# A second matrix product of an MLP by seven block products in place of eight, with the operand sums formed a stage earlier

## The chip, the cores and the metric

The kernel runs on one core of a Trainium2 chip. The metric is the device time of one execution in microseconds. All arithmetic results are float32; each large product is formed from float32 numbers that are split into a rounded part ("hi") and a remainder ("lo"), so that one 128x128 weight block against 128x512 tokens costs three matmuls: hi by hi, hi by lo, lo by hi.

## The reference, cut to what matters

The layer is a hybrid encoder (state-space heads and windowed attention), followed by an MLP. Only the MLP is touched. T is 2048 tokens, the model width 1024, the MLP width 4096:

```python
h = rmsnorm(x, norm_mlp_pre[i])
f = jnp.square(jax.nn.relu(h @ w_up[i])) @ w_down[i]
x = x + rmsnorm(f, norm_mlp_post[i])
```

## The kernel before

Activations lie transposed, features on the 128 partitions and tokens along the free axis. Tokens go in two halves `hf` of 1024, each of two blocks `b` of 512 (`TB`). The MLP has two stages.

The first product, `up`, runs for 2 halves times 16 units `p`. A unit computes two blocks of 128 MLP features for both token blocks. It is a 2x2 by 2x2 block product done with seven products (`PROD`: 1, 5, 6, 3, 7, 2, 4) of 12 matmuls each, whose partial results are chained in three PSUM banks x, y and z (`BANK`). `up_weights` makes the weights of each product: four raw loads for a unit, four of the seven weights formed by an add or subtract (`combine`; the letters of `wcmb='vvp'` say that two in three go to VectorE and one to GpSimd), then a cast to hi on ScalarE and a subtract to lo on VectorE. `up_input` forms the token operands of a half in the same way (`bcmb`, `blo`), in 16 slots of the tag "a" and 16 units of the tag "u". After its eviction each of the four results of a unit is squared (Relu, then Square, on ScalarE) and stored to the DRAM tensor `dff` by the queue of SyncE (SP).

The second product, `down`, runs for 2 halves times 4 quarters `qt` of the MLP width. For each of 8 output blocks `j` and both token blocks one `gemm` of 24 matmuls goes into a bank of the pool "g" (2 banks), and is then added on VectorE to `facc[j]` (copied by ScalarE in the first quarter). `ff_input` loads 16 tiles of `dff` for a quarter through five staging buffers (`stage`: two of tag "gl", three of tag "ld"), casts them to hi and subtracts to lo. Weights come through `wchunk`, two 256 KB chunks for each `j`. In the last quarter of a half `sqadd` adds up the squares of `facc` (ScalarE square, VectorE add), and `facc` is multiplied by `norm_mlp_post`. `final` then forms the norm and the residual and stores the output; for the first half it runs as a side task (`finals`) beside the first quarter of the second half. The very last quarter runs in three parts (`LAST`).

The order of TensorE is written out by hand: `drive` advances a clock of its own by 512/2400 us for a matmul and interleaves the main generator with side generators. The other engines' queues (SP, ScalarE, VectorE, GpSimd) are ordered by the framework's scheduler, and each runs its queue in order on the chip. A tile whose tag has no free buffer makes its first writer wait. Weights of a product are held in 4 buffers of the tag "ws". The tag "ct" has 5 buffers for results of `up`, "nt" has 4 and serves `sqadd` and the norms.

After half 1's normalisation begins (`post`), the units 0 to 3 of half 0 of `up` run beside the residual and norm work of the earlier stage, which uses "gl", "ld" and GpSimd.

Of the kernel before, what the change touches and what calls it, by code (L numbers as in the profile page):

```python
# [8 lines left out]
F32 = mybir.dt.float32  # L9
# [6 lines left out]
P = 128  # L16
D = 1024
# [20 lines left out]
class Layer:  # L38
    def __init__(self, ctx, tc, a, out):
# [24 lines left out]
        self.d_ff = d("dff", [32, P, T])  # L64
# [836 lines left out]
    def sqadd(self, acc, b, t, pool, tag):  # L901
        nc = self.nc
        if acc[b] is None:
            acc[b] = pool.tile([P, TB], F32, tag=tag, name=tag, bufs=2)[:, :t.shape[-1]]
            nc.scalar.activation(acc[b], t, AF.Square)
        else:
            q = self.nt("sq")[:, :t.shape[-1]]
            nc.scalar.activation(q, t, AF.Square)
            nc.vector.tensor_add(acc[b], acc[b], q)
# [53 lines left out]
    def up_weights(self):  # L963
# [3 lines left out]
        def load(p):  # L967
            raw = {}
            for i in range(2):
                for k in range(2):  # L970
                    t = raw[f"{i + 1}{k + 1}"] = self.pw.tile([P, 4, P], F32, tag="raw", name="wu", bufs=8)
                    nc.sync.dma_start(t, self.a["w_up"][2 * p + i, k])
            return raw
# [69 lines left out]
    def up(self, hf, p, B, ws):  # L1043
# [37 lines left out]
    def ff_input(self, hf, qt, ff, after):  # L1081


        nc = self.nc
        for b in range(2):
            for kt in range(8):
                if kt % 4 == 0 and after[b][kt // 4]:
                    yield self.until(after[b][kt // 4])
                x = self.stage(self.d_ff[8 * qt + kt, :, self.tok(hf, b)], kt)
# [3 lines left out]
                yield K["ff_prep"]  # L1093
            self.flags.add(f"ff{hf}{qt}{b}")
# [34 lines left out]
    def finals(self, parts, facc, facs):  # L1129
        for p, c in zip(parts, facs):  # L1130
            yield from self.final(0, p, facc, c, None, 0)

    def final(self, hf, part, facc, acc, xs, wait):
# [59 lines left out]
    def main(self):  # L1193
# [130 lines left out]
        ff = [[None, None] for _ in range(8)]  # L1324
        for hf in range(2):
            for p in range(16):
                if p == 8:
                    self.side(self.r2(hf))
                if p == 15:
                    if hf == 0:  # L1330
                        self.side(self.up_input(1, B[1]))
                    else:
                        self.side(self.ff_input(0, 0, ff, (("uB5", "uB6"), (None, "uB1"))))
# [4 lines left out]
        self.worder = [("w_down", j, (2 * qt, 2 * qt + 1)) for _ in range(2) for qt in range(4) for j in range(8)]  # L1338
        s6.close()
        self.pf, s7 = self.pool("f", "left", 8)  # L1340
        both = ((0, 0, TB), (1, 0, TB))
        for hf in range(2):
            facc = None
            for qt in range(4):
                yield self.until(f"ff{hf}{qt}0", f"ff{hf}{qt}1")
                if facc is None:
                    new = lambda: (self.unit("u", "facc", F32) if hf else
                                   self.pf.tile([P, 2, TB], F32, tag="f", name="facc"))
                    if hf:
                        self.side(self.finals(both, fa, facs))  # L1350
                    facc = [new() for _ in range(8)]
                cur, ff = ff, [[None, None] for _ in range(8)]
                n = (hf, qt + 1) if qt < 3 else (hf + 1, 0)
                if n[0] < 2:
                    self.side(self.ff_input(*n, ff, ((None, None), (f"dn{hf}{qt}1", None))))
                if qt == 3 and hf == 1:
                    ws, xs = [], None
                    yield self.until("fin000", "fin010")
                    for part in self.LAST:
                        facs = [None]  # L1360
                        yield from self.down(qt, cur, facc, (part,), facs, ws)
                        self.side(self.final(1, part, facc, facs[0], xs, K["fin_lag"]))
                        if xs is None:
                            xs = []
                            for j in range(8):
                                xs.append(self.unit("a", "x2", F32)[:, 0])
                                nc.sync.dma_start(xs[j], self.d_x2[j, :, self.tok(1, 1)])
                else:
                    facs = [None, None]
                    yield from self.down(qt, cur, facc, both, facs, None, f"dn{hf}{qt}")  # L1370
            fa = facc
# [85 lines left out]
```

## Time and profile before

| quantity | us |
|---|---|
| median of 3 runs | 3263.02 |
| range of these runs | 3262.8 to 3265.16 |
| profiled execution | 3271.05 |
| span of the profiled execution | 3269.3 |
| TensorE busy in the span | 3024.7 (93%) |
| VectorE busy | 1935.8 (59%) |
| ScalarE busy | 1457.4 (45%) |
| GpSimd busy | 844.6 (26%) |

The span runs from the first to the last instruction; 1.75 us lie around it. A stretch of 40 or of 20 us is better than the whole for judging a stage: `up` runs from about 1828 to 2523 us of the span, `down` from 2523 to about 3253 us. PEclk is the granted TensorE clock as a share of full speed. Since matmuls are pipelined, a busy share of TensorE says little; the count of matmuls in a stretch says more.

### The profile page before, as it was taken

How to read it: one execution, taken by the hardware profiler on the slowest of the kernel's cores; microseconds unless marked ns; L12 is line 12 of the kernel's file. 1: busy time of each engine (PE TensorE's matmuls, PEld its weight loads, DVE VectorE, ACT ScalarE, POOL GpSimd, SP SyncE). 2: the span in 40 equal slices, each digit the busy share in tenths (PEclk: the TensorE clock that was granted, in tenths of full speed). 3: DMA queues.
4: the chain of work that ended last, by engine and by line, in shares of the span. 5: the costliest groups of instructions: out<-in, count | busy, mean ns of one | idle time of the engine just before them, and what ended most of it. 6: DMA issues, size and time to landing. Idle time of an engine off the chain costs nothing. (4 is left out here: it accounts for less than half of the span.)

```text
span 3269.3 us, 40235 instructions
## 1 busy us (share of the span) xinstructions
PE 3024.7 (93%) x13896; PEld 2419.4 (74%) x13896; DVE 1935.8 (59%) x3292; ACT 1457.4 (45%) x2718; POOL 844.6 (26%) x710
## 2 busy tenths in 40 slices
PE   7989999999998899997988869999999999999996
PEld 6778887778886666674766658877888788877886
DVE  7365455557756689958778864565455333553346
ACT  3235566657765545322232545655566322332222
POOL 4242222222234345564536520022000000010001
PEclk9999999999999989997998989999999999999998
DMA  6767544464567655655348473332333422354323
GB/s 227 235 202 205 149 127 116 128 209 138 149 202 249 206 146 152 184 176 163 106 134 263 127 225 107 119 126 87 118 118 128 129 92 87 100 153 124 100 85 97
DMA packets 368955, 489.49 MB, mean 150 GB/s; under 512 B 30192, under 2 KB 198128, under 8 KB 368752
## 3 DMA queue, kind: packets, MB, share of 16 engines
q1 hardware_dynamic: 334128, 451.27, 46.0%
q10 hardware_dynamic: 34624, 35.66, 3.1%
q8 instruction: 110, 1.80, 0.2%
q14 instruction: 93, 0.76, 0.1%
HBM read 330.95 MB, written 155.86 MB: 149 GB/s over the span
## 5 line engine op out<-in xcount | busy, mean ns | idle before, releaser
L86 PE MATMUL psg<-ff,ws 128*128 128x512 f32 (+1 forms) x2760 | 626.1, 389 | 10.2 <-ACT facc L1105 9.0
L86 PEld LDWEIGHTS psg<-ff,ws 128*128 128x128 f32 x2760 | 515.3, 188 | 120.6 <-ACT facc L1105 11.9
L86 PE MATMUL psg<-h,ws 128*128 128x512 f32 x1920 | 486.4, 399 | 19.8 <-ACT z L470 18.0
L86 PEld LDWEIGHTS psg<-h,ws 128*128 128x128 f32 x1920 | 356.7, 190 | 93.7 <-issue 18.7
L84 PE MATMUL psmx<-b,ws 128*128 128x512 f32 x1152 | 297.0, 407 | 41.3 <-DVE c L1078 13.4
L218 POOL TENSOR_SCALAR ws<-wr 128x512 fp32r<-128x512 f32 x184 | 125.4, 682 | 749.2 <-PE psg L86 584.6
L84 PEld LDWEIGHTS psmx<-b,ws 128*128 128x128 f32 x1152 | 224.2, 196 | 98.9 <-ACT c L1075 9.4
L86 PE MATMUL psg<-hr,ws 128*128 128x512 f32 x960 | 250.4, 401 | 5.1 <-DMA hr<-dh 4.4
L221 POOL TENSOR_TENSOR ws<-wr,ws 128x512 fp32r<-128x512 f32 x184 | 250.0, 1359 | 14.7
L86 PE MATMUL psg<-ga,ws 128*128 128x512 f32 x768 | 209.0, 424 | 28.4 <-DVE mix L893 12.3
L777 DVE CUSTOM_DVE_ANT_0 p<-psqk,pack,sinks 128x384 f32<-128x384 f32 (+1 forms) x256 | 152.1, 596 | 139.0 <-PE psqk L86 138.4
L1153 POOL TENSOR_TENSOR facc<-facc,x 128x512 f32<-128x512 f32 (+1 forms) x20 | 24.5, 1223 | 753.8 <-DVE facc L1152 707.7
L86 PE MATMUL psg<-ya,ws 128*128 128x512 f32 x768 | 214.1, 420 | 3.3 <-DVE ya L201 3.2
L86 PEld LDWEIGHTS psg<-hr,ws 128*128 128x128 f32 x960 | 177.2, 190 | 42.3 <-DMA hr<-dh 7.3
L86 PEld LDWEIGHTS psg<-ga,ws 128*128 128x128 f32 x768 | 149.2, 199 | 77.4 <-issue 13.3
L220 ACT CAST ws<-wr 128x512 fp32r<-128x512 f32 x114 | 71.0, 623 | 287.7 <-PE psg L86 263.7
L86 PEld LDWEIGHTS psg<-ya,ws 128*128 128x128 f32 x768 | 143.0, 194 | 45.1 <-issue 14.9
L1107 DVE TENSOR_TENSOR facc<-facc,psg 128x512 f32<-128x512 f32 (+1 forms) x104 | 67.0, 645 | 176.0 <-PE psg L86 175.8
L788 ACT ACTIVATE p<-p,m 128x384 f32<-128x384 f32 (+1 forms) x256 | 151.3, 594 | 36.8 <-DVE m L783 36.7
L206 ACT CAST pt<-pspt 128x512 fp32r<-128x512 f32 x184 | 107.2, 584 | 123.7 <-PE pspt L90 106.3
L221 DVE TENSOR_TENSOR ws<-wr,ws 128x512 fp32r<-128x512 f32 x114 | 78.7, 691 | 137.5 <-ACT ws L220 137.3
L207 DVE TENSOR_TENSOR pt<-pspt,pt 128x512 fp32r<-128x512 f32 x184 | 125.6, 684 | 53.7 <-ACT pt L206 53.3
(224 smaller groups left out, 5512.9 us busy)
## 6 DMA issues: line engine op xcount, KB each, us to landing
wu<-w_up_dram SPq DMA_DIRECT2D x128, 256.0 KB, 2.9
wr<-w_down_dram SPq DMA_DIRECT2D x128, 256.0 KB, 2.6
dff<-c SPq DMA_DIRECT2D x128, 256.0 KB, 2.5
stg<-dff SPq DMA_DIRECT2D x128, 256.0 KB, 3.9
wr<-w_in_dram SPq DMA_DIRECT2D x120, 256.0 KB, 2.8
k<-dk SPq DMA_DIRECT2D x56, 384.0 KB, 4.7
dq<-qst SPq DMA_DIRECT2D x64, 256.0 KB, 3.7
q<-dq SPq DMA_DIRECT2D x64, 256.0 KB, 5.0
```

Of the source, the lines that this page charges most:

```text
L84: self.nc.tensor.matmul(out, lhsT, rhs, start=False, stop=stop, skip_group_check=True)
L86: self.nc.tensor.matmul(out, lhsT, rhs, start=start, stop=stop)
L206: self.nc.scalar.copy(hi, src)
L207: self.nc.vector.tensor_sub(lo, src, hi.bitcast(F32))
L218: self.nc.gpsimd.tensor_scalar(w[:, 0], raw, 1.0, 0.0, ALU.mult, ALU.add)
L220: self.nc.scalar.copy(w[:, 0], raw)
L221: eng.tensor_sub(w[:, 1], raw, w[:, 0].bitcast(F32))
L777: nc.vector.tensor_tensor_reduce(out=p[:, :W], in0=ps[:, :W], in1=bias, scale=1.0, scalar=self.sinks[:, hd:hd + 1], op0=ALU.add, op1=ALU.m ...
L788: nc.scalar.activation(p4[r][:, :W], p4[r][:, :W], AF.Exp, bias=m[:, 0, r:r + 1], scale=float(np.float32(SLOPES[hd])), accum_out=m[:, 2, r ...
L1107: nc.vector.tensor_add(f, f, ps)
L1153: (nc.gpsimd if j % 2 else nc.vector).tensor_add(f, f, x)
```

## The change

Seven of the eight pairs (half, quarter) of the second product are now done by seven products in place of eight. A quarter is a 2x2 block product: two halves `k` of its 1024 features, two interleaved sets `i` of output blocks, two token blocks `b`. For each of the seven products and each of four `p` there are 12 matmuls with one 512-wide weight tile, and an eviction into one of the 32 blocks of `facc`. The partial results stay in PSUM across products, so an accumulating bank is read after each product. Four X chains use the pool of six banks, the Y chains the two banks of the pool "g", hence the split order of products 5 and 3 in `DPH`.

The operand combinations of the tokens are formed in `up`: GpSimd makes four subtractions for a unit, and seven tiles for a unit are stored to a new tensor `dop` (four to `dff` before). The last quarter of half 1 (units 12 to 15) stores only to `dff`, as before, and is computed as before. The combinations of weights are formed once in a side task `w_sums` that starts after unit 3 of half 0: 16 rounds of four loads, four GpSimd operations and four stores to `dws`. `up` takes its weight columns in another order, so that a unit holds features j and j+4 of a quarter.

`down_weights` loads two weight tiles at a time (512 KB) through 8 buffers of the pool "f", and makes hi and lo of each. `down_input` loads 28 operand tiles for a pair and makes hi and lo of each. `facc` of half 0 moves from the pool "f" to the units "u". The adds of squares in the last quarter of half 0 go to GpSimd. The multiplication by `norm_mlp_post` for half 0 moves from `down`'s eviction into `final`, there fused with the multiplication by the norm.

```diff
-        self.d_ff = d("dff", [32, P, T])
+        self.d_op = d("dop", [2, 7, 16, P, TB])
+        self.d_ff = d("dff", [8, P, TH])
+        self.d_ws = d("dws", [4, 4, 4, P, TB])
...
+        last = hf == 1 and p >= 12
         def done(c, i, b, src=None):
             nc.scalar.activation(c, c if src is None else src, AF.Relu)
             nc.scalar.activation(c, c, AF.Square)
-            nc.sync.dma_start(self.d_ff[2 * p + i, :, self.tok(hf, b)], c)
+            if last:
+                nc.sync.dma_start(self.d_ff[4 * i + p - 12, :, b * TB:(b + 1) * TB], c)
+        def op(m, t):
+            nc.sync.dma_start(self.d_op[hf, m - 1, p], t)
...
+            if m == 7:
+                op(3, c[5])
+            elif m == 2:
+                op(1, c[1])
+                t1, t2 = self.ld(name="t1"), self.gl("t2")
+                nc.gpsimd.tensor_sub(t1, c[6], c[1])
+                op(5, t1)
+                nc.gpsimd.tensor_sub(t2, c[5], t1)
+                op(6, t2)
+                nc.gpsimd.tensor_sub(c[6], c[5], c[6])
+                op(7, c[6])
+            elif m == 4:
+                op(2, c[4])
+                t4 = self.ld(name="t4")
+                nc.gpsimd.tensor_sub(t4, c[4], t2)
+                op(4, t4)
+    def w_sums(self):
+        for qt in range(4):
+            for p in range(4):
+                a = {}
+                for i in range(2):
+                    for k in range(2):
+                        t = a[f"{i + 1}{k + 1}"] = self.nt("wsum")
+                        nc.sync.dma_start(t.rearrange("p (k c) -> p k c", k=4), self.a["w_down"][2 * p + i, 2 * qt + k])
+                yield 6
+                for m, fn, x, y, o in ((5, "tensor_add", "21", "22", "21"), (6, "tensor_sub", "21", "11", "11"),
+                                       (7, "tensor_sub", "22", "11", "22"), (3, "tensor_sub", "12", "11", "12")):
+                    getattr(nc.gpsimd, fn)(a[o], a[x], a[y])
+                    nc.sync.dma_start(self.d_ws[(5, 6, 7, 3).index(m), qt, p], a[o])
+                yield 22
+    DPH = ((1, (0, 1, 2, 3)), (5, (0, 1)), (3, (0, 1)), (5, (2, 3)), (3, (2, 3)), (6, (0, 1, 2, 3)), (7, (0, 1, 2, 3)),
+           (2, (0, 1, 2, 3)), (4, (0, 1, 2, 3)))
+    DIN = (1, 5, 3, 6, 7, 2, 4)
+    def down_weights(self):
...
+                        raw = self.pf.tile([P, 2, 4, P], F32, tag="f", name="wd", bufs=8)
...
+                        nc.sync.dma_start(raw, src)
+                        for x in range(2):
+                            w = self.wp.tile([P, 2, 4, P], F32R, tag="ws", name="ws", bufs=4)
+                            nc.scalar.copy(w[:, 0], raw[:, x])
+                            self.eng("wlo").tensor_sub(w[:, 1], raw[:, x], w[:, 0].bitcast(F32))
+                            yield w
+    def down_input(self):
+        done = ["uB5", "uB6", "uB3", "uB7"]
...
+                for m in self.DIN:
+                    yield self.until(done.pop(0))
+                    done.append(f"D{hf}{qt}{m}")
+                    B = self.B2[hf, qt, m] = []
+                    for i in range(4):
+                        x = self.stage(self.d_op[hf, m - 1, 4 * qt + i], i)
+                        t = self.slot("ff")
+                        nc.scalar.copy(t[:, 0], x)
+                        self.eng("flo").tensor_sub(t[:, 1], x, t[:, 0].bitcast(F32))
+                        B.append(t)
+                        yield 1.5
+    def down_fast(self, hf, qt, facc, acc, ws):
+        first, final = (1, 5, 3, 4), (6, 7, 2, 4)
+        out = {1: ((0, 0),), 5: ((1, 1),), 3: ((0, 1),), 6: ((0, 1),), 7: ((1, 1),), 2: ((0, 0),), 4: ((1, 0),)}
+        for m, ps_ in self.DPH:
+            yield self.until(f"I{hf}{qt}{m}")
...
+            for p in ps_:
+                w = next(ws)
+                more = m not in (1, 5, 2)
+                if m == 1:
+                    X[p] = self.ps("psx")
+                elif m in (5, 2):
+                    Y[p] = self.pg.tile([P, TB], F32, tag="g", name="psy")
+                ps = X[p] if m in (1, 6, 7, 4) else Y[p]
...
+                f = facc[2 * p + i][:, b]
+                if qt == 0 and m in first:
+                    nc.scalar.copy(f, ps)
+                else:
+                    nc.vector.tensor_add(f, f, ps)
+                if qt == 3 and m in final:
+                    self.sqadd(acc, b, f, self.pf, "facs", nc.gpsimd)
...
             f = facc[j][:, b, c0:c1]
-            nc.vector.tensor_mul(f, f, r)
+            if scale:
+                nc.vector.scalar_tensor_tensor(f, f, self.vec["norm_mlp_post"][:, j:j + 1], r, ALU.mult, ALU.mult)
+            else:
+                nc.vector.tensor_mul(f, f, r)
...
+            facc, facs = [self.unit("u", "facc", F32) for _ in range(8)], [None, None]
+            for qt in range(3 if hf else 4):
+                if (hf, qt) == (1, 2):
+                    ff = [[None, None] for _ in range(8)]
+                    self.side(self.ff_input(ff, ((("I124", "D126"), ("D127",)), (("fin000", "fin010"), ()))))
+                yield from self.down_fast(hf, qt, facc, facs, wsa)
+        yield self.until("ff0", "ff1")
```

## Rows read from the trace of the kernel before

**Rows 1.** The page, busy time, share of the span and instructions of each engine.

```profile
PE 3024.7 (93%) x13896; PEld 2419.4 (74%) x13896; DVE 1935.8 (59%) x3292; ACT 1457.4 (45%) x2718; POOL 844.6 (26%) x710
```

**Rows 2.** Windows by stage: stretch, its us, busy us (instructions) by engine, PEclk, DMA, GB/s.

```profile
core 0: us, PE busy (x) PEld busy (x) DVE busy (x) ACT busy (x) POOL busy (x), PEclk, DMA share, GB/s
1828.00:1959.00 131.00, 94.48 (x343) 72.65 (x342) 93.07 (x112) 62.94 (x108) 44.92 (x29) 0.86 0.60 183
1959.00:2158.00 199.00, 197.69 (x869) 162.67 (x868) 95.41 (x140) 116.44 (x193) 17.25 (x14) 1.00 0.35 117
2158.00:2237.00 79.00, 64.47 (x244) 48.58 (x243) 62.83 (x70) 44.34 (x81) 35.18 (x23) 0.91 0.33 107
2237.00:2523.00 286.00, 284.50 (x1251) 234.28 (x1250) 139.15 (x207) 169.43 (x285) 23.24 (x18) 1.00 0.33 112
2523.00:2560.00 37.00, 35.17 (x153) 28.06 (x152) 17.86 (x28) 20.78 (x38) 0.00 (x0) 1.00 0.74 234
2560.00:2872.00 312.00, 312.00 (x1378) 258.37 (x1377) 116.70 (x181) 77.37 (x132) 0.00 (x0) 1.00 0.30 91
2872.00:2947.00 75.00, 67.87 (x286) 54.03 (x286) 42.63 (x60) 25.02 (x39) 11.99 (x8) 0.98 0.56 169
2947.00:3148.00 201.00, 199.72 (x881) 165.04 (x880) 70.94 (x107) 47.73 (x81) 0.00 (x0) 1.00 0.34 101
```

**Rows 3.** Chain of work, one product of 12 matmuls: start us, us, what.

```profile
2079.44 2.72 PE psmy L86 x12
```

**Rows 4.** Groups of instructions in `down`, 2560 to 2872 us: busy us, mean ns.

```profile
L221 DVE TENSOR_TENSOR ws<-wr,ws 128x512 fp32r<-128x512 f32 x57 | 39.4, 692 | 77.4 <-ACT ws L220 77.3
L220 ACT CAST ws<-wr 128x512 fp32r<-128x512 f32 x58 | 36.2, 624 | 150.0 <-PE psg L86 149.9
L1107 DVE TENSOR_TENSOR facc<-facc,psg 128x512 f32<-128x512 f32 x47 | 32.3, 687 | 94.2 <-PE psg L86 94.2
L1092 DVE TENSOR_TENSOR ff<-stg,ff 128x512 fp32r<-128x512 f32 x49 | 32.3, 690 | 18.3 <-ACT ff L1091 18.3
```

**Rows 5.** Windows of 20 us, columns as in rows 2: two bursts of input in `down`.

```profile
2780.00:2800.00 20.00, 20.00 (x90) 16.55 (x89) 13.61 (x22) 10.06 (x18) 0.00 (x0) 1.00 0.74 238
3060.00:3080.00 20.00, 20.00 (x90) 16.57 (x89) 12.96 (x21) 8.54 (x16) 0.00 (x0) 1.00 0.79 247
```

**Rows 6.** Timeline of `up` in its steady part: start us, us, engine, line, [idle before].

```profile
2084.72 2.88 PE L84 MATMUL psmy<-b,ws 128*128 128x512 f32 x12
2087.64 0.69 DVE L1078 TENSOR_TENSOR c<-c,psmy 128x512 f32<-128x512 f32 x1 [0.89 <-PE psmy L84]
2090.41 0.63 ACT L984 CAST ws<-wc 128x512 fp32r<-128x512 f32 x1 [0.75 <-PE psmx L84]
```

**Rows 7.** Source L960, weight sums of `up`: duration ns min/median/max on GpSimd and VectorE.

```profile
L960 DVE TENSOR_TENSOR wc<-wu x44: 678/693/1785, 1779.2 to 2500.0; 128x512 f32<-128x512 f32 x44
L960 POOL TENSOR_TENSOR wc<-wu x20: 1283/1297/1744, 1863.8 to 2462.0; 128x512 f32<-128x512 f32 x20
```

**Rows 8.** Timeline at the turn of halves in `up`.

```profile
2202.17 1.71 POOL L1038 TENSOR_TENSOR b<-x,b 128x512 fp32r<-128x512 f32 x1
2202.68 1.75 DVE L1038 TENSOR_TENSOR b<-x,b 128x512 fp32r<-128x512 f32 x1
2207.83 2.93 PE L84 MATMUL psmx<-b,ws 128*128 128x512 f32 x6 [2.92 <-DVE b L1038]
```

**Rows 9.** Chain and TensorE's timeline early in `up`.

```profile
1944.64 5.46 DMA mix<-dmix
1953.89 5.21 PE L84 MATMUL psmx<-b,ws 128*128 128x512 f32 x12 [6.05 <-DVE c L1078]
```

**Rows 10.** Timeline of `down`'s beginning, TensorE.

```profile
2547.08 3.26 PE L86 MATMUL psg<-ff,ws 128*128 128x512 f32 x13 [1.32 <-ACT facc L1105]
```

**Rows 11.** Waits from 2872 to 2950 us: us in total, times, longest.

```profile
PE psg L86 <- ACT facc L1105: 7.1, 4, 3.8
SPq L1154 <- POOL facc L1153: 22.6, 8, 6.0
```

More of the change, by code (lines that the diff above doesn't have):

```diff
@@ L1079, in up @@
                 done(c[o], i, b)
-    def ff_input(self, hf, qt, ff, after):
+            if last:
+                continue
+            if m == 7:
[14 more added lines that the diff above has]
+                op(4, t4)
@@ new lines, in w_sums @@
+    def w_sums(self):
+        nc = self.nc
+        for qt in range(4):
[11 more added lines that the diff above has]
+                yield 22
@@ new lines, in down_input @@
+    def down_input(self):
+        nc = self.nc
+        done = ["uB5", "uB6", "uB3", "uB7"]
+        for hf in range(2):
+            for qt in range(3 if hf else 4):
+                for m in self.DIN:
[9 more added lines that the diff above has]
+                        yield 1.5
+                    self.flags.add(f"I{hf}{qt}{m}")
@@ new lines, in down_fast @@
+    def down_fast(self, hf, qt, facc, acc, ws):
+        nc = self.nc
+        X, Y = {}, {}
+        first, final = (1, 5, 3, 4), (6, 7, 2, 4)
+        out = {1: ((0, 0),), 5: ((1, 1),), 3: ((0, 1),), 6: ((0, 1),), 7: ((1, 1),), 2: ((0, 0),), 4: ((1, 0),)}
+        for m, ps_ in self.DPH:
+            yield self.until(f"I{hf}{qt}{m}")
+            if (hf, qt, m) == (1, 2, 4):
+                yield self.until("ff0")
+                self.wsend()
+            B = self.B2[hf, qt, m]
+            for p in ps_:
[6 more added lines that the diff above has]
+                ps = X[p] if m in (1, 6, 7, 4) else Y[p]
+                for k in range(4):
+                    s = B[k]
+                    self.mm(ps, w[:, 0, k], s[:, 0], k == 0, False, more)
+                    self.mm(ps, w[:, 0, k], s[:, 1], False, False, more)
+                    self.mm(ps, w[:, 1, k], s[:, 0], False, k == 3, more)
+                    if k % 2:
+                        yield
+                if p == ps_[-1] and (p == 3 or m not in (5, 3)):
+                    self.flags.add(f"D{hf}{qt}{m}")
+                (i, b), = out[m]
+                f = facc[2 * p + i][:, b]
[5 more added lines that the diff above has]
+                    self.sqadd(acc, b, f, self.pf, "facs", nc.gpsimd)
@@ L1084, in ff_input @@
+    def ff_input(self, ff, after):
         nc = self.nc
@@ L1086, in ff_input @@
             for kt in range(8):
-                if kt % 4 == 0 and after[b][kt // 4]:
-                    yield self.until(after[b][kt // 4])
-                x = self.stage(self.d_ff[8 * qt + kt, :, self.tok(hf, b)], kt)
+                if kt % 4 == 0:
+                    yield self.until(*after[b][kt // 4])
+                x = self.stage(self.d_ff[kt, :, b * TB:(b + 1) * TB], kt)
                 t = ff[kt][b] = self.unit("au"[b], "ff")
@@ L1092, in ff_input @@
                 self.eng("flo").tensor_sub(t[:, 1], x, t[:, 0].bitcast(F32))
-                yield K["ff_prep"]
-            self.flags.add(f"ff{hf}{qt}{b}")
+                yield 1.5
+            self.flags.add(f"ff{b}")
     def down(self, qt, ff, facc, parts, acc=None, ws=None, flag=None):
@@ L1130, in finals, with final @@
         for p, c in zip(parts, facs):
-            yield from self.final(0, p, facc, c, None, 0)
-    def final(self, hf, part, facc, acc, xs, wait):
+            yield from self.final(0, p, facc, c, None, 0, True)
+    def final(self, hf, part, facc, acc, xs, wait, scale=False):
         nc = self.nc
@@ L1323, in main @@
         wsa = ahead(K["w_ahead"])
-        ff = [[None, None] for _ in range(8)]
+        self.B2 = {}
         for hf in range(2):
@@ L1337, in main @@
                     s3.close()
-        self.worder = [("w_down", j, (2 * qt, 2 * qt + 1)) for _ in range(2) for qt in range(4) for j in range(8)]
+                    self.side(self.w_sums())
+        self.worder = [("w_down", j, (6, 7)) for j in range(8)]
         s6.close()
@@ L1341, in main @@
         both = ((0, 0, TB), (1, 0, TB))
+        ws, wq = self.down_weights(), []
+        wsa = ahead(K["w_ahead"])
         for hf in range(2):
[L1343 to L1370, printed above, removed]
@@ L1371, in main @@
-            fa = facc
+            if hf:
+                self.side(self.finals(both, facc, facs))
+            facc, facs = [self.unit("u", "facc", F32) for _ in range(8)], [None, None]
+            for qt in range(3 if hf else 4):
+                if (hf, qt) == (1, 2):
+                    ff = [[None, None] for _ in range(8)]
+                    self.side(self.ff_input(ff, ((("I124", "D126"), ("D127",)), (("fin000", "fin010"), ()))))
+                yield from self.down_fast(hf, qt, facc, facs, wsa)
@@ new lines, in main @@
+        yield self.until("ff0", "ff1")
+        ws, xs = [], None
+        for part in self.LAST:
+            facs = [None]
+            yield from self.down(3, ff, facc, (part,), facs, ws)
+            self.side(self.final(1, part, facc, facs[0], xs, K["fin_lag"]))
+            if xs is None:
+                xs = []
+                for j in range(8):
+                    xs.append(self.unit("a", "x2", F32)[:, 0])
+                    nc.sync.dma_start(xs[j], self.d_x2[j, :, self.tok(1, 1)])
```

17 lines of the change are left out of this document (13 added, 4 removed).

## The prediction

> **What bounds the kernel now.** I read the page's busy shares first [rows 1]: TensorE 93%, VectorE 59%, ScalarE 45%, GpSimd 26%. These are means over unlike stages, so the second view is the windows by stage [rows 2]. There the reader should count matmuls, not busy time, since the ends of matmuls are modelled. The third view, the chain of work, gives the pace: 12 matmuls take 2.72 us [rows 3], so 0.2267 us each. With that, each stretch splits into matmuls and time lost. From 2560 to 2872 us, `down` runs 1378 matmuls: 1378 x 0.2267 = 312.4 us in a stretch of 312 us. Nothing is lost; TensorE's count of matmuls alone sets the time. From 2947 to 3148 us it is 881, or 199.7 of 201 us. The two quiet parts of `up` are the same: 869 matmuls make 197.0 of 199 us, 1251 make 283.6 of 286 us. What is lost stands in four stretches. Early in `up`, 343 matmuls make 77.8 us of 131, so 53 are lost. At the turn of halves in `up`, 244 make 55.3 of 79, so 24 are lost. At the start of `down`, 153 make 34.7 of 37, so 2 are lost. At its turn of halves, 286 make 64.8 of 75, so 10 are lost. So `down` is bound by TensorE but for some 12 us, and `up` has two holes in which other engines or transfers set the pace. The change takes matmuls out of the first and puts work into the second.
>
> **What is removed.** A pair of half and quarter has 8 x 2 gemms of 24 matmuls, 384. Seven products by four by 12 are 336. Over seven pairs 336 matmuls go: 336 x 0.2267 = 76.2 us. A pair should take 336 x 0.2267 = 76.2 us too, in place of 87.1. The 2.72 us of a product with a weight tile of its own is already reached in `up` [rows 3], where each product has 12 matmuls, one weight tile and one eviction as well.
>
> **What `down` gains in other work.** Weight tiles, input tiles and evictions each rise from 16 to 28 for a pair. On VectorE a tile's remainder takes 0.692 us for a weight and 0.690 for an input, and an add from PSUM 0.687 [rows 4]. So VectorE has 28 x (0.692 + 0.690 + 0.687) = 57.9 us in 76.2, or 76%. ScalarE has two casts of about 0.62 us [rows 4] for each product, 28 x 1.25 = 35 us, 46%. Transfers are 56 x 256 KB = 14.7 MB in 76.2 us, 193 GB/s. Rows near this: two bursts in `down` in which VectorE was busy 13.61 and 12.96 of 20 us (68% and 65%), at 238 and 247 GB/s, and TensorE still ran 90 matmuls, its full count [rows 5]. So the transfers lie inside what was shown; VectorE lies 8 points beyond, for long and not for 20 us. The new point of danger is PSUM. Before, a bank had 24 matmuls, 5.44 us, before it was wanted again. Now eight of the 28 products of a pair (3 and the second part of 5, and two of product 2) want the bank that was read out only one product earlier, 2.72 us. The add must be done by then. In `up` VectorE begins 0.04 us after the modelled end of the matmuls it waited for [rows 6] and needs 0.69, so two foreign VectorE operations (1.38 us) fit ahead of it, not three. Cost: between 0 and, if half an operation too many stands ahead at each of the 56 places, 56 x 0.35 = 20 us. I take 3: the weights are ready early (four buffers; the cast of rows 6 waits for a product to end, so preparation is as far ahead as the buffers allow), inputs are asked for some ten products ahead, and in a first quarter 16 of 28 evictions are ScalarE's.
>
> **What `up` gains.** Each unit but the last four stores seven tiles, not four, and GpSimd does four subtractions: 28 x 4 = 112, and `w_sums` 64 more. At 1.29 us [rows 7] that is 176 x 1.29 = 227 us of GpSimd in a stage of 695 us in which it was busy 121 [rows 2]. Transfers rise by 0.79 MB for a unit, and by 2.1 MB for each round of `w_sums` (28 us of the kernel's own clock), so from 117 to about 117 + 41 + 72 = 230 GB/s, within rows 5. GpSimd's queue holds the sums for a third of the weights too (`wcmb`). An operation that waits for the squares of product 2 holds these back, but a weight is some three products, 8 us, ahead. A result buffer of "ct" is kept longer: that of product 1 by a subtraction and a store, about 3 us of the 8 it has. In the quiet 485 us I count 0 to 20 us, and take 4, since a burst of four operations from `w_sums` is 5.2 us long and only some of 16 bursts meet a weight or a buffer that is due.
>
> GpSimd also slows VectorE. A VectorE sum in SBUF takes 0.69 us, at most 1.785 [rows 7]. At the turn the one of 1.75 us lies beside a GpSimd operation of 1.71, and TensorE waits 2.92 us for the next remainder [rows 8]. So a GpSimd operation costs VectorE up to 1.06 us. The Trainium skill says (SBUF — State Buffer, Who interferes with whom) that VectorE with two SBUF inputs and GpSimd contend for one pair of ports, as an exclusive lock, and that the loser blocks; the trace agrees, 0.69 against 1.75 us. By that rule the change's use of GpSimd is no free use of an idle engine; its result here is the third rival below.
>
> **At the turn of halves in `up`** VectorE is busy 62.8 and GpSimd 35.2 of 79 us [rows 2], and both form the operands that TensorE waits for. About three units' subtractions (12) and nearly three rounds of `w_sums` (11) fall there: 23 x 1.29 = 30 us more for GpSimd, 23 x 1.06 = 24 us more for VectorE. Cost 0 (if all fall where nobody waits) to 28 us. I take 14, half, because some of it is due only when TensorE has got on.
>
> **Early in `up`** TensorE's losses follow the loads of `mix` [rows 9], which go round in two "gl" buffers; t2 of each unit now wants one of them, and t1 and t4 want "ld". Four units, about 5 us of a buffer each, over two buffers: 10 us more for that chain, of which TensorE now loses 53 of 131, 40%. With three more stores for a unit and 16 GpSimd operations, 0 to 25 us; I take 6.
>
> **The ends of `down`.** At the start TensorE waits for an eviction by ScalarE that stood behind late inputs [rows 10]. That goes, as the first four inputs are asked for earlier, but the first weights now need a 512 KB load into memory that `up` gives back, where they had a buffer of their own. From -2 (what is lost now) to 8, the time of a load and its preparation: 3. At the turn of halves TensorE loses 10 us, 7.1 of them to evictions by ScalarE, and SP's queue stands 22.6 us behind stores that wait for GpSimd [rows 11]. Now this queue carries 1.75 times the inputs and weights, and `final` shares "ld" with the inputs; behind SP's waiting stores stand loads of weights and inputs, behind these ScalarE's casts. The adds of squares on GpSimd (14) cost VectorE up to 15 us just before. Against that weights can be 16 products ahead and inputs ten. -9 (all of it hidden) to 20: 7. The last quarter's 16 input tiles must come in the last 12 products: 0 to 5, 1. The moved `norm_mlp_post` takes 16 scalings off VectorE and adds none, the new column order and the place of `facc` cost nothing: TensorE hides both.
>
> **The sum**: -76.2 + 6 + 14 + 4 + 3 + 3 + 7 + 1 = -38.2 us. On the profiled execution (span 3269.3, with what lies around it 3271.05) that gives 3232.9. The median of the runs is 8.0 us below this, so 3225. The unknowns are independent; adding their distances to the upper ends as squares gives about 36 us, to the lower ends 23 us: 3202 to 3261 for this case.
>
> **Rivals.** First, the added work hides: all positive terms are near zero, and the gross gain stays, 3263 - 76 = 3187, some microseconds more for the ends, 3190. For it speaks that both quiet stages lose nothing at present and have half of VectorE free; against it the two holes, where the new work meets engines that are late.
>
> Second, slower: the eviction becomes the bound. If VectorE's queue, at 76% with inputs in bursts of four, lets each of the 56 tight places wait for two operations more than fit (1.38 us), 56 x 1.38 = 77 us in place of 3: 3225 + 74 = 3299. It decides against the change from (38.2 + 3) / 56 = 0.74 us at each place, one operation too many. For it: the shorter time between uses of a bank, and inputs that a late transfer can put ahead of an add. Against it: full pace at 68% in rows 5, and 20 of 28 products have no tight bank.
>
> Third, the ports: GpSimd's 176 operations take VectorE's time in all of `up`. If a third of 176 x 1.06 = 187 us comes through to TensorE, that is 62 us in place of the 24 taken, 3225 + 38 = 3263, no change. Against it: in the quiet part VectorE is busy 95 of 199 us [rows 2], 9.1 for a unit of 19.0; a unit gets four operations and some 2.3 of `w_sums`, 6.7 us, and 15.8 still fit.
>
> **How the numbers follow.** Forecast 3225 with 0.60, the first rival 3190 with 0.17, the second 3299 with 0.13, the third 3263 with 0.10. About 0.2%, 6.5 us, is what a measurement of this kernel can tell from no change. The forecast's case is faster but for 0.03; the first is faster; the second slower; of the third 0.04 is faster, 0.03 the same, 0.03 slower. So faster 0.78, the same 0.05, slower 0.17. The range 3185 to 3275 holds the forecast, the first rival and most of the third; it leaves out the second and some tails, 0.18.
>
> **What would show it.** After: 336 matmuls fewer; in `down`'s quiet parts 90 matmuls in 20 us, with VectorE near 15 of 20. If TensorE waits there for adds from PSUM, the second rival holds. In `up`, the stretch at the turn longer than 79 us by some 14, with more VectorE operations of 1.75 us; if the quiet part loses 2 us or more for a unit, the third. The prediction is wrong if weights, not evictions, hold `down`, or if the holes of `up` grow by more than 45 us.

## The result, and the profile after

The changed kernel takes 3300.58 us (median of 4 runs, 3297.75 to 3302.96) against 3264.07 for the kernel before: ratio 1.0112, 95% interval 1.0094 to 1.0129. It is slower by about 36 us; 3225 was forecast, so the forecast's direction was wrong. The two profiled executions, from which the traces come, lie closer: 3271.05 and 3297.75 us, so the balances below are of 26.7 us.

First the page's busy times, to be held against [rows 1]: TensorE has less to do, VectorE and GpSimd more, and the span is longer.

```profile
PE 2973.0 (90%) x13560; PEld 2369.2 (72%) x13560; DVE 2167.4 (66%) x3514; ACT 1555.7 (47%) x2886; POOL 1132.7 (34%) x900
```

336 matmuls are gone, as reckoned (13896 to 13560). Then the windows by stage (columns as in [rows 2]); the first five lie in `up`, the last three in `down`:

```profile
1822.00:1958.00 136.00, 94.14 (x344) 72.35 (x343) 94.09 (x110) 64.17 (x110) 64.04 (x42) 0.86 0.58 193
2079.00:2221.00 142.00, 116.30 (x474) 93.41 (x474) 76.26 (x75) 59.86 (x103) 87.68 (x60) 0.90 0.61 218
2221.00:2299.00 78.00, 50.99 (x174) 36.68 (x173) 61.54 (x58) 35.06 (x65) 61.52 (x41) 0.80 0.48 169
2299.00:2420.00 121.00, 121.00 (x536) 100.19 (x535) 73.23 (x82) 66.96 (x114) 52.56 (x36) 1.00 0.45 158
2420.00:2600.00 180.00, 167.11 (x717) 135.87 (x716) 97.98 (x128) 101.83 (x171) 58.34 (x41) 0.97 0.50 171
2647.00:2910.00 263.00, 263.00 (x1162) 217.78 (x1161) 190.54 (x285) 125.48 (x209) 12.62 (x10) 1.00 0.61 195
2910.00:3010.00 100.00, 81.92 (x332) 63.99 (x331) 69.07 (x104) 46.19 (x76) 18.70 (x13) 0.95 0.67 207
3010.00:3174.00 164.00, 163.92 (x723) 135.11 (x722) 121.87 (x188) 79.87 (x135) 0.00 (x0) 1.00 0.61 193
```

`down` does what was reckoned: 1162 matmuls x 0.2267 us are 263.4 us in a stretch of 263, nothing lost, with VectorE busy 72%. The loss is in `up`. From 2079 to 2221 us, with units that ran at full pace before, 474 matmuls make 107 us of 142; from 2299 to 2420 us nothing is lost, though GpSimd's subtractions go on there (it is busy 52.56 us, none of it with weight sums). At the turn of halves in `down`, 332 matmuls make 75 us of 100.

Three marks from TensorE's timeline give the balance: the first matmul of `up`, the first of `down`'s seven pairs, the first of the last quarter. `up`, up to `down`'s first matmul and so with the wait for `down`'s first weights, went from 695.2 to 789.7 us (+94.5), the seven pairs from 625.2 to 562.7 (-62.5), what lies ahead and behind by -5.3: +26.7 in span.

A unit of `up` has 84 matmuls, 19.0 us at full pace. Measuring from each unit's product 2 to the next shows which units are late (us, worked out from TensorE's timelines; 1 to 16 belong to half 0 and the turn; e5, e9, e12 and e15 are experiments below; unit 0 has no product 2 before it):

```
unit     before  after     e5     e9    e12    e15
 1        26.0   27.7   27.7   27.7   29.3   27.7
 2        35.6   44.0   44.1   43.9   42.4   45.0
 3        31.1   34.0   33.1   33.6   34.0   33.6
 4        27.6   20.1   19.1   26.4   19.1   19.1
 5        19.0   27.8   19.0   19.0   19.0   19.0
 6, 7     38.1   38.1   38.1   38.1   38.6   38.8
 8        20.8   26.0   25.7   25.7   32.2   27.3
 9        20.6   19.8   20.5   30.6   25.3   19.2
10        19.0   31.1   19.0   40.5   19.4   19.0
11        19.0   20.5   19.0   19.0   20.2   19.0
12        19.0   20.8   19.0   19.0   19.0   19.0
13        19.0   33.9   19.0   19.0   20.1   19.9
14        19.0   23.8   19.0   19.0   19.0   19.5
15        19.0   19.0   19.0   19.0   19.0   19.0
16, 17    62.2   77.2   63.9   64.3   74.0   64.8
18 to 23 114.2  114.2  114.2  114.2  115.5  114.7
24, 25    41.4   46.3   46.8   57.1   56.5   48.2
26, 27    38.1   48.7   38.1   38.1   38.1   38.1
28 to 31  76.2   76.2   76.2   76.2   76.2   80.0
```

TensorE's waits, 1820 to 2580 us (us in total, times, longest), then ScalarE's and GpSimd's, 1960 to 2240 us:

```profile
PE psmy L86 <- ACT c L1083: 54.4, 14, 11.8
PE psmx L86 <- ACT c L1083: 19.4, 6, 5.3
...
ACT c L1083 <- POOL c L1100: 52.7, 9, 15.5
ACT c L1083 <- DMA dop<-c: 11.0, 4, 4.9
...
POOL wsum L1121 <- DMA wsum<-w_down_dram: 53.9, 7, 9.6
```

L1083 is the eviction copy into a result buffer of "ct", L1100 the third subtraction of the unit before, which holds that buffer, and L1121 a weight sum. The worst place in the timeline (start us, us, [idle before <- what ended it]):

```profile
2157.33 6.12 POOL L1121 TENSOR_TENSOR wsum<-wsum 128x512 f32<-128x512 f32 x4 [6.41 <-DMA wsum<-w_down_dram]
2163.85 2.55 SPq L1117 DMA_DIRECT2D wsum<-w_down_dram  x4
2170.56 2.60 POOL L1121 TENSOR_TENSOR wsum<-wsum 128x512 f32<-128x512 f32 x2 [7.11 <-DMA wsum<-w_down_dram]
2174.34 1.26 POOL L1096 TENSOR_TENSOR t<-c,c 128x512 f32<-128x512 f32 x1
2178.90 1.71 POOL L1100 TENSOR_TENSOR c<-c,c 128x512 f32<-128x512 f32 x1
2180.64 0.59 ACT L1083 COPY c<-psmy 128x512 f32<-128x512 f32 x1 [15.46 <-POOL c L1100]
2181.28 2.93 PE L86 MATMUL psmy<-b,ws 128*128 128x512 f32 x6 [11.80 <-ACT c L1083]
```

Product 2 of this unit is added at 2158.6 us, so the subtractions are due at about 2161. GpSimd is then in a round of weight sums until 2163.45, its queue has the next round in front of them, and that round's loads are issued only at 2163.85. It stands idle for 7.11 us, with a subtraction behind it whose inputs have been there since about 2161. The first subtraction (L1096) comes 13 us late, the buffer is free at 2180.6, ScalarE has stood 15.46 us and TensorE 11.80.

### The profile page after: what moved, and what is told of

Read it like the earlier page. It is cut to its first block, busy times and chain, and to the rows that moved or that the text cites. A ratio compares the mean times of both kernels' runs of the same rounds, so it can differ in the third digit from the quotient of the medians.

```text
span 3296.0 us, 40950 instructions
## 1 busy us (share of the span) xinstructions
PE 2973.0 (90%) x13560; PEld 2369.2 (72%) x13560; DVE 2167.4 (66%) x3514; ACT 1555.7 (47%) x2886; POOL 1132.7 (34%) x900
## 5 line engine op out<-in xcount | busy, mean ns | idle before, releaser
L86 PE MATMUL psmx<-b,ws 128*128 128x512 f32 x1152 | 304.1, 415 | 41.1 <-ACT c L1083 19.4
L86 PE MATMUL psx<-ff,ws 128*128 128x512 f32 x1008 | 233.9, 392 | 7.8 <-DVE ws L1148 7.7
L86 PEld LDWEIGHTS psx<-ff,ws 128*128 128x128 f32 x1008 | 190.4, 189 | 49.1 <-DVE ws L1148 9.1
L1147 ACT CAST ws<-wd 128x512 fp32r<-128x512 f32 x196 | 121.9, 623 | 215.4 <-PE psx L86 93.4
L987 DVE TENSOR_TENSOR ws<-wc,ws 128x512 fp32r<-128x512 f32 x128 | 132.8, 1039 | 56.4 <-ACT ws L986 56.0
L1148 DVE TENSOR_TENSOR ws<-wd,ws 128x512 fp32r<-128x512 f32 x196 | 137.1, 701 | 38.1 <-ACT ws L1147 37.8
L88 PE MATMUL psy<-ff,ws 128*128 128x512 f32 x672 | 156.7, 390 | 1.7 <-DVE facc L1205 1.2
```

The costliest lines, as they stand in the source:

```text
L86: self.nc.tensor.matmul(out, lhsT, rhs, start=False, stop=stop, skip_group_check=True)
L88: self.nc.tensor.matmul(out, lhsT, rhs, start=start, stop=stop)
L987: self.eng("wlo").tensor_sub(w[:, 1], x, w[:, 0].bitcast(F32))
L1147: nc.scalar.copy(w[:, 0], raw[:, x])
L1148: self.eng("wlo").tensor_sub(w[:, 1], raw[:, x], w[:, 0].bitcast(F32))
```

## The experiments

Three theories were put up. **A**: GpSimd's in-order queue; weight sums in a row, some of them waiting for their loads, hold back the subtractions, these hold the result buffers, and so the evictions and TensorE. **B**: GpSimd's operations slow VectorE through the shared port, in proportion to their number. **C**: the added bytes. The times are medians, the ratios are to the kernel before as measured beside each. Its median was then 3267.1 to 3269.2 us, 3 to 5 us above that in the result, so a difference of that size between one experiment and another, or the changed kernel, says little.

**Each half of the added work taken away.** e1, no weight sums (no `self.side(self.w_sums())`; plain weight tiles in their place):

> Leaves out the forming of the weight sums: products 5, 6, 7 and 3 of the second product take plain weight tiles in place of sums, in the same number of loads of the same size. Gone are 64 loads, 64 stores and 64 GpSimd operations in the stage of the first product. The changed kernel takes 3300.6 us, 84 us longer than before in that stage up to its last matmul. Theory A (one queue behind another: GpSimd stands at its weight sums until their loads land, the operand subtractions stand behind them, a result buffer stays taken, ScalarE's eviction copy and then TensorE wait): most of the loss in the quiet part of the stage goes, 3235 to 3255 us, and the waits of TensorE on the eviction copy (54 us on bank y) fall below 15 us. Theory B (GpSimd takes VectorE's time through a shared port, in proportion to operations): 64 of 176 go, so about 30 of 84 us, 3270 us. Theory C (more bytes): 34 of 73 MB added to that stage go, so some 40 us, 3260 us, but the turn of halves stays as it is.

3234.9 us, ratio 0.992 (0.989 to 0.995), at the fast end of A's range. `up` took 719.2 us. e2, no subtractions:

```diff
-                nc.gpsimd.tensor_sub(t1, c[6], c[1])
-                op(5, t1)
+                op(5, c[6])
...
```

> Leaves out the four operand subtractions of each unit; the same seven stores are made, of tiles that are there anyway. The weight sums stay on GpSimd. Theory A: a result buffer no longer waits for GpSimd, so its blocking at the weight sums reaches TensorE only through a third of the weight combinations; most of the loss goes, 3225 to 3250 us. Theory B: 112 of 176 GpSimd operations go, 53 of 84 us, 3247 us, which doesn't tell A from B here but does together with the run without weight sums: by B the two gains stand as 64 to 112 and add up, by A each alone brings most of it. Theory C: nothing changes, 3300 us.

3251.3 us, 1 us above A's range; `up` 735.6. e3, neither of the two:

> Leaves out both the weight sums and the operand subtractions. What is left of the change is the seven-product form of the second product, with its weights, inputs and evictions, and three more stores for a unit. By theories A and B the stage of the first product is then near its length before (695 us, plus 0 to 10 for the stores and 11 for the wait for the first weights): 3205 to 3220 us, which is the gross gain of the second product as measured in the trace (63 us) less these. Theory C: still 25 to 40 us longer in the stage of the first product, 3235 to 3250 us.

3221.1 us; `up` 702.5, of which 11.0 are the wait for the first weights. Beyond e3 the subtractions alone cost `up` 16.7 us, the weight sums alone 33.1, both 87.2. They don't add up, which speaks for A and against B. Nor does the changed kernel's price come through the subtractions alone: weight sums without any subtraction (e2) still cost the quiet units 22 us, subtractions without weight sums (e1) 9 us, both together 63. By which path e2's 22 us arise was not singled out. C falls for the stores: in e3 the quiet units take what they took before (212.8 and 269.9 us), so the three stores more for a unit cost nothing.

**More buffers.** e4: seven "ct" buffers in place of five, six "raw" in place of eight.

> The whole computation, with seven result buffers of the first product in place of five and six raw weight buffers in place of eight, so that the memory is the same. Theory A: a late subtraction no longer stops the eviction of the next unit but only that after it; TensorE's waits on the eviction copy fall from 54 us on bank y to below 25 us, 3255 to 3275 us. Theory B: no change in GpSimd's operations, so no change, 3300 us, or slower by the weights' shorter lead. Theory C: 3300 us.

3280.8 us: 20 us gained, 6 us short of A's range (3255 to 3275), and not none, as B has it. TensorE's waits for the copy on bank y are gone from the head of the list; 28.3 us for weight remainders (L987) stand there; GpSimd's queue also holds weight combinations.

**Which part of a weight sum costs.** e5 keeps its loads and stores and leaves out GpSimd's operations (its output is made from plain weight tiles):

> Leaves out the 64 GpSimd operations of the weight sums and keeps their 64 loads and 64 stores, which now store plain tiles; the operand subtractions stay on GpSimd. Theory A (GpSimd stands in its queue at the weight sums until their loads land): as without the whole side task, 3235 to 3245 us. Theory C (bytes, or loads in SP's queue behind stores): the side task costs as before, 3285 to 3300 us. In between, e.g. 3265, each has its share.

3237.9 us, as without the side task. From 1960 to 2150 us of the span in e1 (first) and in e5:

```profile
1960.00:2150.00 190.00, 185.88 (x808) 151.86 (x807) 112.33 (x132) 109.38 (x182) 76.56 (x53) 0.99 0.45 154
```

```profile
1960.00:2150.00 190.00, 186.00 (x808) 151.93 (x807) 111.27 (x132) 107.68 (x179) 73.66 (x51) 0.99 0.75 260
```

808 matmuls in both, at 154 and at 260 GB/s: C is out. e9 does the reverse: the 64 operations on a constant tile, without loads and with a quarter of the stores.

> Leaves out the weight sums' loads, and 48 of their 64 stores; the 64 GpSimd operations stay, of the same size and with two inputs in SBUF, but on a constant tile that is always there, so that GpSimd never waits for a load (the second product takes plain weights). The run without the side task took 3234.9 us, the one with its transfers alone 3237.9, the changed kernel 3300.6. Theory A1 (what costs is that GpSimd stands still until loads have landed, with the subtractions behind it): near the runs without operations, 3236 to 3250 us. Theory A2 (what costs is the queue's length: bursts of four operations, 5.2 us, ahead of the subtractions) or theory B (their occupation of the port against VectorE): 3275 to 3300 us, with GpSimd hardly waiting for transfers.

3283.0 us, in the range that A2 and B share, so waiting for loads was not the whole of it. But e9 does not say how much of the changed kernel's loss the waiting was: with nothing to wait for, the scheduler puts the operations in longer rows than there:

```profile
2088.18 31.94 POOL L1122 TENSOR_TENSOR wsum<-pack 128x512 f32<-128x512 f32 x28
```

Units 9 and 10 take 30.6 and 40.5 us, the five after them 19.0, with all subtractions on GpSimd.

**Later operations.** e6: pauses of 16 in place of 6 behind the loads, 12 in place of 22 behind a round (us of the kernel's own clock, `yield`).

> The whole computation; the four GpSimd operations of a round of weight sums are put 16 us of the kernel's own clock behind their loads, not 6, and the next round 12 behind them, not 22. Same operations, same bytes. Theory A: GpSimd finds the loads landed; its waits on them (68 us from 1950 to 2240 us of the span) fall below 20 us, and the time to 3245 to 3270 us. Theories B and C: the same count of GpSimd operations and bytes, 3295 to 3305 us.

3302.0 us, nothing gained. A's expectation failed because the edit did not do what I took it to do: the rounds stood where they had stood (2087, 2101, 2124, 2145, 2165 us; 2080, 2094, 2116, 2138, 2157 in the changed kernel, whose `up` begins 6 us earlier in its span), and GpSimd's waits for transfers at the sums stayed at 68 us (1950 to 2240 us). So the pauses in this side generator do not place GpSimd's operations. That the scheduler fills that queue as data and buffers come free fits this, and was not looked into further.

**Subtractions on VectorE** (e7):

> The whole computation, with the four operand subtractions of a unit on VectorE in place of GpSimd. Theory A: they no longer stand behind GpSimd's weight sums, so a result buffer comes free in time; near the run without subtractions (3251 us), 3250 to 3270 us, with TensorE's waits on the eviction copy down from 74 to below 30 us. Theory B: 112 fewer GpSimd operations but 112 x 0.69 = 77 us more for VectorE; part of 53 us is gained, 3265 to 3290 us.

3258.0 us, ratio 0.997 (0.996 to 0.999), in A's range and below B's (from 3265); now 52 us of ScalarE's waits are for stores of result buffers.

**First weights early** (e8: two tiles loaded one unit earlier, into the "wr" buffers):

> The whole computation; only the first two weight tiles of the second product are loaded one unit earlier, into two weight buffers that are idle then. In the changed kernel TensorE waits 10.9 us there. If that wait is the load alone: 8 to 10 us are gained, 3290 to 3293 us. If the cast on ScalarE stands behind late inputs anyway: 0 to 3 us.

3300.5 us. The first two products ran at once, and the wait of 8 us came at the third: the loads behind them wait for memory that `up` gives back with its last stores.

**Combined** (e10: e7, seven buffers, four products' weights loaded early into two free tiles of "u"; e11: also `wcmb='v'`):

> The whole computation: subtractions on VectorE (3258.0 us alone), seven result buffers and six raw weight buffers (19.8 us gained on the changed kernel alone), and the first two loads of second-product weights (four products) put one unit earlier into two units that are free then. In the run with subtractions on VectorE ScalarE's eviction copy waited 52 us in all for a store of a result buffer; theory A says that seven buffers take most of this away and that the wait of 11 us at the start of the second product goes: 3215 to 3235 us. Theory B: VectorE's added 77 us and GpSimd's weight sums stay: 3245 to 3258 us.

> As the run before it, and the third of the first product's weight combinations that GpSimd makes goes to VectorE too, so that nothing that TensorE waits for in the quiet part stands behind the weight sums. Theory A: the last path from GpSimd's queue to TensorE in the quiet part is cut, 5 to 12 us faster than the run before it. Theory B: VectorE gets 42 operations of 0.69 us more, 29 us, and is the bound: the same or up to 10 us slower.

3243.2 us (0.993) and 3225.4 us (ratio 0.987, 0.985 to 0.989). e10 lies between A's range (to 3235) and B's (from 3245); the step to e11 was 18 us, more than A's 5 to 12 and opposite to B. In e10 GpSimd's queue still had weights for TensorE behind the weight sums.

**The rounds put in place.** Still open was whether the place of the operations or their number costs. e12 queues each round's four operations behind the last subtraction of one unit, by an order-only edge (it fixes the order of two instructions in a queue and carries no data):

```diff
-                yield 6
+                yield self.until(units[4 * qt + p])
+                behind = getattr(self.t4, "ins", self.t4)
...
+                    with self.tc.issue_after(behind):
+                        getattr(nc.gpsimd, fn)(a[o], a[x], a[y])
```

> The whole computation; the changed kernel's GpSimd operations and transfers all stay, but the four weight-sum operations of a round are queued on GpSimd behind the last subtraction of one unit each: units 5 to 14 of half 0 and 2 to 7 of half 1, none at the turn of halves. Theory A (bunching: operations in a row, some of them waiting for loads, hold GpSimd's queue when a subtraction is due): units of the quiet part return from up to 33.9 to 19 to 20 us, the turn loses 6 us of its 15, and the time falls from 3300.6 to 3235 to 3255 us. Theory B (176 operations take VectorE's time through the port, wherever they stand): the loss is spread, not gone, 3285 to 3300 us.

3272.3 us: 28 gained, between the two expectations. The table of units shows where: units 10 to 14 took 130.0 us in the changed kernel, 97.7 here (95.2 at full pace). But units 8 and 24, in which the norm `r2` runs, take 32 and 34 us; TensorE waits 20.2 us for r2's load. The rounds beside it hold "nt" buffers, which is the likely reason, not a shown one. e13 (with seven buffers and early weights) and e14 (and `wcmb='v'`) kept that wait:

> As e12, with seven result buffers and six raw weight buffers, and the first two loads of second-product weights put one unit earlier into free units. Theory A: the buffers have nothing more to mend in the quiet part, 0 to 4 us; the wait of 11 us at the start of the second product goes, as its four products cover the load: 8 to 11 us faster than e12, 3225 to 3245 us. If the wait only moves to the fifth product, the same as e12.

> As e13, with the third of the first product's weight combinations that GpSimd makes put on VectorE. In the run with bunched rounds this step brought 18 us. Theory A: with one round for a unit there is no bunch to escape from, so 0 to 4 us. If weight combinations stand behind a round in each unit anyway (a burst of 5.2 us, a lead of 8 us): 5 to 15 us faster.

3252.6 and 3246.7 us, 20 and 26 us below e12, and e13's step is larger than the 8 to 11 expected; the step of 6 us to e14 is too small beside the spread of its runs (3241.6 to 3255.3) to decide between its two expectations. e15 moves nothing but places: loads behind the last store of the unit before, operations behind the last subtraction of their unit, no round in the units of r2 or at the turn.

> The whole computation, as the changed kernel, but each round of weight sums has its unit: its loads are queued on SP behind the last store of the unit before, its four GpSimd operations behind the last subtraction of its own unit; units 4, 5, 6, 9 to 13 of half 0 and 2 to 6, 9 to 11 of half 1, so none in the units with the norm r2 (7, 8) and none at the turn. Theory A (place in the queues and held buffers): units 8 and 24 fall from 32 and 34 us in e12 to 21 to 25, all other quiet units 19 to 20; 3240 to 3255 us. Theory B (the number of operations): as e12, 3272 us.

3242.5 us, ratio 0.993 (0.991 to 0.995): 58 us faster than the changed kernel with the same operations and bytes. Units 8 and 24 fall to 27.3 and 27.5 us, not to the 21 to 25 expected; in e5, without these operations, they take 25.7 and 25.2. From 2087 to 2200 us, with five rounds inside (columns as in [rows 2]; one round of it below):

```profile
2087.00:2200.00 113.00, 108.90 (x478) 89.19 (x476) 78.41 (x81) 59.27 (x104) 76.63 (x52) 1.00 0.69 245
```

```profile
2125.93 1.75 POOL L1105 TENSOR_TENSOR t<-c,t 128x512 f32<-128x512 f32 x1
2127.64 1.29 POOL L1129 TENSOR_TENSOR wsum<-wsum 128x512 f32<-128x512 f32 x1
2128.89 1.29 POOL L962 TENSOR_TENSOR wc<-wc,wu 128x512 f32<-128x512 f32 x1
2130.13 4.69 POOL L1129 TENSOR_TENSOR wsum<-wsum 128x512 f32<-128x512 f32 x3
2143.02 1.30 POOL L962 TENSOR_TENSOR wc<-wu 128x512 f32<-128x512 f32 x1 [8.20 <-DVE ws L987]
2144.28 1.29 POOL L1096 TENSOR_TENSOR t<-c,c 128x512 f32<-128x512 f32 x1
```

GpSimd is busy 68% here, VectorE 69%, and 478 matmuls make 108.4 of 113 us. In the changed kernel GpSimd was busy 62% from 2079 to 2221 us, and 35 us were lost. B is out as the cause of the quiet part's loss: more work of the same kind in the same time costs 5 us if it stands in the right place. VectorE is even slowed more here. These are its remainders of combined and of raw weights (count, busy us, mean ns), in the changed kernel from 2079 to 2221 us, then in e15 from 2087 to 2200 us:

```profile
L987 DVE TENSOR_TENSOR ws<-wc,ws 128x512 fp32r<-128x512 f32 x23 | 26.6, 1158 | 9.2 <-ACT ws L986 8.9
L987 DVE TENSOR_TENSOR ws<-wu,ws 128x512 fp32r<-128x512 f32 x18 | 17.4, 973 | 12.0 <-ACT ws L986 12.0
```

```profile
L987 DVE TENSOR_TENSOR ws<-wc,ws 128x512 fp32r<-128x512 f32 x21 | 23.0, 1097 | 7.5 <-ACT ws L986 7.5
L987 DVE TENSOR_TENSOR ws<-wu,ws 128x512 fp32r<-128x512 f32 x18 | 22.4, 1264 | 1.3 <-ACT ws L986 1.3
```

Over both kinds that is 1.07 us in the mean in the changed kernel, 1.16 in e15. e16 adds the other mends:

> As e15, with seven result and six raw buffers, the first two loads of second-product weights one unit early, and all first-product weight combinations on VectorE. e13 and e14 gained 20 and 26 us on e12 by these. Theory A: the same on e15, 3212 to 3232 us, at or below the fastest so far (3225 us, with subtractions on VectorE).

3224.0 us, ratio 0.987 (0.984 to 0.989), the same as e11. Both beat the kernel before by some 43 us.

## Why the prediction was wrong, step by step

- **The gross gain, 76.2 us, and the pace of `down`**: right. The quiet stretches run at 0.2267 us a matmul, and TensorE's waits for evictions (`facc`) are 2.5 us in all seven pairs, where 3 were taken. VectorE is busy 72%, 76% were reckoned. TensorE's waits from 2611 to 3174 us:

```profile
PE psx L88 <- ACT ws L1147: 10.9, 1, 10.9
PE psx L86 <- DVE ws L1148: 7.7, 2, 6.8
PE psy L86 <- ACT ff L1164: 3.9, 1, 3.9
...
PE psy L86 <- ACT facc L1203: 1.3, 2, 0.7
PE psy L88 <- DVE facc L1205: 1.2, 1, 1.2
```

- **The second rival** (evictions hold `down`) forecast 3299 and the kernel takes 3300.6, but that is chance: its mechanism did not occur.
- **Early in `up`, 6**: units 1 to 4 took 125.8 us, 120.3 before, +5.5. **The turn, 14**: units 16 and 17 took 77.2, 62.2 before, +15.0. Both right in size. Without subtractions units 1 to 4 take 116.8 us (e2), so the 5.5 hang on the subtractions; that the "gl" buffers are the way was not tried. Without weight sums the turn takes 64.2 us (e1), without subtractions 73.2 (e2), so most of its 15 belongs to the weight sums, where the prediction counted about as many subtractions.
- **The quiet part of `up`, 4 (0 to 20)**: this step failed. Units 5 to 15 took 260.7 us, 212.8 before; 18 to 31 took 285.4, 269.9 before: +63.4, where 4 was taken. On the profiled execution -38.2 us was forecast and +26.7 measured, and 59 of these 65 us are this term. Three points of the working were wrong. I took a round's distance from the generator's pauses (28 us); the rounds came 13 to 23 us apart within a row (31 and 34 at the turn), and none began from 2002 to 2079 us or from 2279 to 2465 us. (A round's 2.1 MB in 28 us are also 75 GB/s, not 72; nothing hangs on that.) I gave the result buffer 5 us to spare by counting a subtraction as if GpSimd's queue were empty. And I priced weight sums and subtractions apart, where half of the price is in their meeting (9 and 22 us alone, 63 together). The sentence that a waiting operation holds back what stands behind it was there, with the weights as its victim and not the result buffers, and the weights' 8 us lead was counted against it. In the changed kernel TensorE's waits are for the result buffers (74 us for the copy L1083, 1 us for weight remainders L987); weights come to the front when buffers are added (e4).
- **The third rival** (ports) named the right stage and not the cause: its sign, 2 us or more lost for a unit of the quiet part, came true (63.4 us over 25 units), so the sign could not tell it from a queue. The remainders of combined weights did go from 0.70 to 1.16 us in the mean (1960 to 2150 us; e9 and the changed kernel alike), yet in e15 VectorE is slowed as much and TensorE runs at nearly full pace. That the port has no share in the 15 us of the turn was not tried.
- **The start of `down`, 3 (-2 to 8)**: the wait was 10.9 us, outside the bounds. I priced the load and its preparation; the wait is for memory that the last stores of `up` free (in the changed kernel the weight loads are issued at 2604.8 us, behind the last store, issued at 2604.0; e8 only moves the wait; with four products covered, e10, e13 and e16 have 1.4 to 1.7 us left at the fifth).
- **Evictions, turn of halves and handoff in `down`, 3 + 7 + 1**: its seven pairs hold 533.1 us of matmuls in 562.7, so 29.6 are lost, against 15.9 before by the same count: +13.7 where 11 were taken. Most of it stands at the turn, where 25 of 100 us are lost and 10 of 75 were before: the 7 is the term that was too small, within its bounds, and the longest waits there are for weights (7.7 us, L1148) and inputs (3.9 us, L1164), not for evictions as before.

## What to carry to other kernels

An engine's free share says what work it can take, not when: ask of each operation added to an in-order queue what stands behind it, which buffer that work frees, and who waits for the buffer. Pauses in a generator need not place the work of other engines (e6); where the place matters, tie it with an order-only edge to an instruction that marks the place, away from stretches that already wait. Price two additions to one queue together, not each alone.

## What the runs showed of the hardware

Transfers at 260 GB/s, with the DMA engines busy 0.75 of the time, cost TensorE nothing beside 154 GB/s: 808 matmuls in 190 us either way (e5 and e1). VectorE's weight remainders took 0.70 us in the mean in the quiet part before, 1.16 in e15's stretch with GpSimd busy 68%. A wait has a tail: where TensorE had stood for 7.64 us, the next 12 matmuls took 5.49 us in place of 2.88, and the granted clock from 2106 to 2112 us was 0.50, the lower level of 1.2 GHz.

```profile
2106.04 5.49 PE L86 MATMUL psmy<-b,ws 128*128 128x512 f32 x12 [7.64 <-ACT c L1083]
```

The window of these 6 us, columns as in [rows 2]:

```profile
2106.00:2112.00 6.00, 5.96 (x14) 4.76 (x15) 2.08 (x3) 1.95 (x4) 1.05 (x1) 0.50 0.92 323
```
